# A hybrid decoder layer on one core: two weight staging buffers, another order of the key and query moves, one distance table, sums of squares in the P V pool

## Chip, cores and metric

One core of a Trainium2 chip. The metric is device time of one launch in microseconds (us), the median over runs; lower is better. The profile is of one execution of the kernel.

## The reference, cut to what matters

One layer over 1024 prompt tokens and 8 sampled tokens (one new token each, with key and value caches): an RMS norm, one combined projection to everything that follows, three groups of dilated attention and one sliding-window attention with per-head norms of q and k and an ALiBi penalty, gates, two branch projections, an output projection and a residual.

```python
def project_inputs(x, norm_gain, w_in, qk_norm_a, qk_norm_b):
    h = rms_norm(x, norm_gain)
    parts = jnp.split(jnp.einsum("ntd,de->nte", h, w_in), SPLIT_POINTS, axis=-1)
    ...
def banded_attention(q, k, v, slopes, sinks, max_delta, dist):
    ...
    s = jnp.einsum("nbqgrd,nbkgd->nbgrqk", qb, kk).astype(jnp.float32) * (hd ** -0.5)
    bias = -slopes[:, :, None, None] * (delta * dist)
    p, lse = masked_softmax(s + bias, valid, sink)
    o = jnp.einsum("nbgrqk,nbkgd->nbqgrd", p, vv)
...
# group g of mixer A: windows (128, 512, 2048), dilations (1, 4, 16); weights of the groups from lse
o_a = jnp.einsum("gnth,gnthd->nthd", jax.nn.softmax(lse_a, axis=0), o_a_groups)
a = o_a * silu(z_a); b = o_b * silu(z_b)
mixed = sigmoid(g_a) * (a @ w_branch_a) + sigmoid(g_b) * (b @ w_branch_b)
y = x + mixed @ w_out
```

The caches of the sampled tokens are also written out, shifted by one position.

## The kernel before, in words

The tokens are the columns (1032 of them, in three chunks of 344), features the partitions. Every matrix product in full precision is made of three: both operands are split into a high and a low part (hi and lo), and hi·hi, hi·lo and lo·hi are summed in PSUM. Weights come as 82 tiles of 128 output features (`ORDER`), each 512 KB: 66 of the combined projection, 8 of the branch projections, 8 of the output. `w_load` (L114) has SP load a tile into a staging buffer (`w_st`, one buffer), and `w_conv` (L120) splits it in two halves: ScalarE writes the high part (L126), GpSimd the low part (L127).

A tile and a chunk make a `slot` of 24 matmuls (L248), cut into three *parts* of 8. The program is written in the order of these parts. At the end of each, `part_end` lets the other work in: the attention's three lanes in turn (`stage_s`: S = q·k, L434 or L448/449; `stage_t`: transposes of the probabilities P, L501; `stage_pv`: P V, L543 or L574), everything deferred with `after(parts, f)`, one step of two generators (`dec`, the sampled tokens; `mer`, the combination of the groups), and one piece of the splits of q and k. A unit is one head and some blocks of 128 queries; a job is a pair of heads (head 0, head 1) of a group. Groups 0, 1 and 3 (the sliding window) use `prep_q` and `prep_k`; the third dilated group is `g == 2` and has its own `prep_k2`.

For S, hi and lo of a head are stacked on the partitions: a k tile pair per head (`k_a0`, `k_b0` for head 0, `k_a1`, `k_b1` for head 1), q likewise. The split computes hi and lo for both heads at once, in the rows where they happen to be, and six DMA moves (`move`, L311) of 64 rows each bring the rest to its place. All DMAs (weights, moves, caches, 1 MB copies of the sampled caches at L141, one every six parts) are issued by SP, in program order; a wait of one holds up those behind it.

PSUM has eight banks in three pools: "d" (2) for the dense products, "w" (4) for S, the transposes, sums of squares and small products, "o" (2) for P V. The sum of squares of a q or k chunk (`ssq` in `ev_qk`, L950/951) stays in its bank until `norm` has read it (L230, L960). `evac_o2` empties P V of `g == 2`: two banks, four ScalarE copies (L585/586), two VectorE adds (L590), one GpSimd add (L591). The ALiBi table is loaded per head (`load_tabs`, L1248), and S is turned into penalised scores with it by one VectorE operation (L457, or L437 and L439).

In the main loop the conversion of the next tile and the load of the one after it are placed by hand:

```python
after(1, lambda: w_conv(n + 1, ks=slice(0, 4)))
after(3, lambda: w_conv(n + 1, ks=slice(4, KK)))
after(5, lambda: w_load(n + 2))
```

Of the kernel before, what the change touches and what calls it, by code (L numbers as in the profile page):

```python
# [20 lines left out]
T = 1024  # L21
# [40 lines left out]

def heads(g, c):
    return (2 * c, 2 * c + 1) if g < 3 else (c, 4 + c)
# [3 lines left out]
def hybrid_step(ctx: ExitStack, tc: tile.TileContext, a):  # L68
# [20 lines left out]
    qkg = cst.tile([128, 8], F32, name="qkg")  # L89
    eps = cst.tile([128, 1], F32, name="eps")  # L90
# [6 lines left out]
    nsink = cst.tile([128, 8], F32, name="nsink")  # L97
    nc.vector.memset(eps, EPS)
# [54 lines left out]
    def rt(name):  # L153
        return bp.tile([128, TT], F32R, tag="B", bufs=18, name=name)

    def ft(name):
        return bp.tile([128, TT], F32, tag="B", bufs=18, name=name)
# [45 lines left out]
    def h_root(j):  # L203
        pm = psum("w", 4)
# [108 lines left out]
    def prep_q(j):  # L313

        j.sq = [rt("q_st") for _ in range(2)]
        t = rt("q_lo")
# [19 lines left out]
    def prep_k2(j):  # L336
# [3 lines left out]
        def piece(y):  # L340
            v = j.k[:, :T].rearrange("p (s r) -> p r s", r=16)[:, 8 * y:8 * y + 8].rearrange("p (b w) s -> p b w s", w=2)
            t0, t1 = [side(j.sk[h][y]) for h in range(2)]
            t4 = t0.rearrange("p b l (w s) -> p b l w s", s=64)
            nc.scalar.activation(t4[:, :, 0], v, AF.Copy)
            nc.vector.tensor_tensor(t4[:, :, 1], v, t4[:, :, 0].bitcast(F32), op=ALU.subtract)
# [4 lines left out]
            after(1, lambda: mv(t1, lo_rows, 0, t0, hi_rows, 0))  # L350
            after(1, lambda: mv(t1, hi_rows, 1, t0, hi_rows, 0))
            after(2, lambda: mv(t1, lo_rows, 1, t0, hi_rows, 1))
            after(2, lambda: mv(t1, hi_rows, 0, t0, hi_rows, 1))
            after(5, lambda: mv(t0, hi_rows, 1, t0, lo_rows, 0))
            after(5, lambda: mv(t0, hi_rows, 0, t0, lo_rows, 1))
# [3 lines left out]
    def prep_k(j):  # L359
# [5 lines left out]
        def piece(half):  # L365
            c = part_of(j, half)
            v = j.view(j.k[:, :T])[:, c]
            h = j.view_o(a0[:, :T])[:, c]
            nc.scalar.activation(h, v, AF.Copy)
            nc.vector.tensor_tensor(j.view_o(b0[:, :T])[:, c], v, h.bitcast(F32), op=ALU.subtract)  # L370
            if half:
                after(1, lambda: move(a1, lo_rows, a0, hi_rows))
                after(1, lambda: move(b1, hi_rows, a0, hi_rows))
                after(2, lambda: move(a1, hi_rows, b0, hi_rows))
                after(2, lambda: move(b1, lo_rows, b0, hi_rows))
                after(5, lambda: move(b0, hi_rows, a0, lo_rows))
                after(5, lambda: move(a0, hi_rows, b0, lo_rows))
# [3 lines left out]
    def prep_v(j, half):  # L381
# [3 lines left out]
        pt = psum("w", 4)  # L385
# [36 lines left out]
    def stage_s(u):  # L422
# [3 lines left out]
        if j.g == 2:  # L426
            bias = tab3[:, hd]
            for x in range(2):
                pt = psum("w", 4)
# [8 lines left out]
                for y in range(2):  # L438
                    nc.vector.tensor_tensor_reduce(out=p[:, y], in0=pv[:, y, 0], in1=p[:, y], scale=-0.125, scalar=3e38,  # L439
# [3 lines left out]
        pt = psum("w", 4)  # L443
# [49 lines left out]
    def stage_t(u):  # L493
# [5 lines left out]
        pt = psum("w", 4)  # L499
# [7 lines left out]
        def split():  # L507
            if j.g == 2:

                u.pt = pts[u.base % 3]  # L510
                t = u.pt[:, :T].rearrange("p (b l q) -> p b l q", l=2, q=128)
# [966 lines left out]
```

## Time and profile before

| | us |
|---|---|
| median of three runs | 1244.9 (1244.15 to 1245.51) |
| the profiled execution | 1248.59 |
| its span | 1246.0 |
| TensorE busy (matmul) | 1181.5 |
| ScalarE, VectorE, GpSimd busy | 730.4, 707.0, 606.3 |
| mean granted clock of TensorE | 0.977 of full speed |

The span is the time from the first to the last instruction in the trace of that execution. Busy times of the engines overlap each other. TensorE runs at one of two levels, 2.4 GHz (granted clock 1.00) or 1.2 GHz (0.50).

### The profile page before, as it was taken

The numbers are of one execution on the slowest core, as the hardware profiler recorded it, in microseconds if no ns is written. First come the engines' busy times: TensorE is split into PE (matmuls) and PEld (weight loads), VectorE is DVE, ScalarE is ACT, GpSimd is POOL, SyncE is SP. The second block draws the span as 40 slices with busy tenths as digits, with TensorE's granted clock in tenths as the row PEclk, the third lists the DMA queues.
The fourth block names the chain that finished last, engine by engine and source line by source line (L and its number), as shares of the span: only waits on it lengthen the run. The fifth ranks groups of instructions, "written<-read, shape, count | busy, mean of one in ns | idle before, by whom it ended". The sixth has DMA issues, their size and how long they took to land.

```text
span 1246.0 us, 21929 instructions
## 1 busy us (share of the span) xinstructions
PE 1181.5 (95%) x7625; PEld 1154.4 (93%) x7625; DVE 707.0 (57%) x1714; ACT 730.4 (59%) x1830; POOL 606.3 (49%) x681
## 2 busy tenths in 40 slices
PE   7899999999999998989998989989899999999998
PEld 6799999999899988979987989989899989999998
DVE  5852454676667475766755865757855564333111
ACT  5644675776758584758755677847686522443110
POOL 3554243443535455746363853638554685444220
PEclk9999999999999998989998989989999998999999
DMA  7047557675684849667775859486688754543343
GB/s 224 35 145 224 175 195 223 195 228 149 221 266 166 254 145 279 194 168 220 213 227 177 241 191 264 143 262 195 182 258 228 238 178 161 187 145 110 111 147 100
DMA packets 127278, 238.83 MB, mean 192 GB/s; under 512 B 28648, under 2 KB 102208, under 8 KB 125760
## 3 DMA queue, kind: packets, MB, share of 16 engines
q1 hardware_dynamic: 127168, 237.43, 62.3%
q8 instruction: 60, 0.98, 0.3%
q14 instruction: 50, 0.41, 0.1%
HBM read 180.14 MB, written 113.25 MB: 235 GB/s over the span
## 4 chain that ended last, share of the span: by engine, by line
PE 73%; DMA 7%; DVE 6%; POOL 5%; ACT 4%; issue 4%; SPq 1%; POOLq 0%; DVEq 0%; ACTq 0%
PE ps_d L248 55%; PE ps_w L248 4%; DMA k_a<-k_b 3%; PE ps_w L501 3%; PE ps_o L574 2%; PE ps_w L448 2%; PE ps_w L449 2%; DMA k_b<-k_b 2%; DMA w_st<-in_w 1%; ACT P L467 1%; PE ps_o L248 1%; DVE n_t L726 1%; POOL q_lo L324 1%; POOL n_t L591 1%; PE ps_w L950 1%
## 5 line engine op out<-in xcount | busy, mean ns | idle before, releaser
L248 PE MATMUL ps_d<-h_hi,w 128*128 128x344 f32 x3456 | 867.7, 327 | 12.2 <-DVE sq L1122 5.7
L248 PEld LDWEIGHTS ps_d<-h_hi,w 128*128 128x128 f32 x3456 | 611.7, 193 | 17.1 <-ACT h_hi L191 6.7
L248 PE MATMUL ps_d<-h_lo,w 128*128 128x344 f32 x1728 | 573.2, 332 | 5.9 <-POOL h_lo L221 3.3
L248 PEld LDWEIGHTS ps_d<-h_lo,w 128*128 128x128 f32 x1728 | 332.2, 192 | 10.6 <-POOL h_lo L221 5.8
L127 POOL TENSOR_TENSOR w<-w_st,w 128x512 fp32r<-128x512 f32 (+1 forms) x159 | 211.1, 1330 | 208.3 <-ACT w L126 193.4
L126 ACT ACTIVATE w<-w_st 128x512 fp32r<-128x512 f32 (+1 forms) x160 | 100.3, 631 | 113.3 <-DMA w_st<-in_w 112.5
L467 ACT ACTIVATE P<-P,st 128x256 f32<-128x256 f32 (+1 forms) x256 | 115.6, 453 | 65.6 <-DVE st L457 59.4
L956 POOL TENSOR_TENSOR qn<-qn,rn 128x344 f32<-128x344 f32 x48 | 45.6, 949 | 151.6 <-ACT rn L226 139.7
L528 DVE TENSOR_TENSOR pt<-ps_w,pt 128x384 fp32r<-128x384 f32 (+1 forms) x112 | 49.4, 441 | 57.7 <-ACT pt L527 57.3
L448 PE MATMUL ps_w<-k_a,q_st 128*128 128x128 f32 (+1 forms) x192 | 51.8, 293 | 29.0 <-DMA k_a<-k_b 14.6
L527 ACT ACTIVATE pt<-ps_w 128x384 fp32r<-128x384 f32 (+1 forms) x112 | 44.1, 394 | 42.8 <-DVE pt L528 36.0
L448 PEld LDWEIGHTS ps_w<-k_a,q_st 128*128 128x128 f32 x192 | 37.6, 196 | 31.0 <-issue 31.0
L501 PE MATMUL ps_w<-ident,P 128*128 128x128 f32 x400 | 62.3, 273 | 3.9 <-DVE pt L528 2.1
L956 POOL TENSOR_TENSOR kn<-kn,rn 128x344 f32<-128x344 f32 x39 | 37.0, 949 | 57.0 <-ACT rn L226 51.8
L941 ACT ACTIVATE sq<-ps_d 128x344 f32<-128x344 f32 x87 | 39.3, 452 | 39.8 <-PE ps_d L248 36.2
L946 DVE TENSOR_TENSOR sql<-sq,sqh 128x344 fp32r<-128x344 f32 x87 | 59.5, 684 | 0.8
L457 DVE CUSTOM_DVE_ANT_0 P<-ps_w,tab 128x256 f32<-128x256 f32 (+1 forms) x128 | 43.4, 375 | 27.4 <-PE ps_w L449 27.2
L501 PEld LDWEIGHTS ps_w<-ident,P 128*128 128x128 f32 x400 | 50.2, 140 | 7.1 <-issue 2.3
L792 POOL TENSOR_TENSOR dkv<-dkv,qb 128x512 f32<-128x512 f32 x32 | 42.4, 1331 | 28.0 <-DMA dkv<-in_ca 9.5
L1174 DVE TENSOR_TENSOR xres<-ps_d,xres 128x344 f32<-128x344 f32 x24 | 12.4, 517 | 76.1 <-PE ps_d L248 44.9
L230 DVE SCALAR_TENSOR_TENSOR ps_w<-ps_w,rt 128x344 f32<-128x344 f32 x87 | 45.2, 520 | 18.0 <-ACT rt L227 17.7
L449 PE MATMUL ps_w<-k_b,q_st 128*128 128x128 f32 (+1 forms) x192 | 53.1, 287 | 0.0
(226 smaller groups left out, 2064.7 us busy)
## 6 DMA issues: line engine op xcount, KB each, us to landing
w_st<-in_w SPq DMA_DIRECT2D x81, 512.0 KB
out_sa<-in_ca SPq DMA_DIRECT2D x16, 1020.0 KB
dkv<-in_ca SPq DMA_DIRECT2D x24, 512.0 KB
q_st<-q_lo SPq DMA_DIRECT2D x32, 256.0 KB
k_st<-k_st SPq DMA_DIRECT2D x48, 128.0 KB
sc<-sc_dr SPq DMA_DIRECT2D x32, 192.0 KB
k_b<-k_a SPq DMA_DIRECT2D x18, 256.0 KB
k_a<-k_b SPq DMA_DIRECT2D x18, 256.0 KB
```

Source lines behind the costliest of these rows:

```text
L126: nc.scalar.activation(wh, s, AF.Copy)
L127: eng.tensor_tensor(wl, s, wh.bitcast(F32), op=ALU.subtract)
L230: nc.vector.scalar_tensor_tensor(ssq, ssq, n * EPS, t, op0=ALU.add, op1=ALU.mult)
L248: nc.tensor.matmul(pt[:, :CH], ops[i][0], ops[i][1], start=(i == 0), stop=(i == N - 1))
L448: nc.tensor.matmul(pt[:, o:o + 128 * nk], j.sq[h][:, q], j.ka[h][:, k], start=True, stop=False)
L449: nc.tensor.matmul(pt[:, o:o + 128 * nk], j.sq[h][:, q], j.sk[h][:, k], start=False, stop=True)
L467: nc.scalar.activation(u.p[:, c], u.p[:, c], AF.Exp, scale=-1.0, bias=st[:, qb, h:h + 1], accum_out=st[:, qb, 2 + h:3 + h])
L501: nc.tensor.transpose(pt[:, o:o + 128], u.p[:, o:o + 128], ident)
L527: nc.scalar.activation(t[:, p0:p0 + m], pt[:, o:o + m], AF.Copy)
L528: nc.vector.tensor_tensor(t[:, 512 + p0:512 + p0 + m], pt[:, o:o + m], t[:, p0:p0 + m].bitcast(F32), op=ALU.subtract)
L946: after(0, lambda: nc.vector.tensor_tensor(sl, s, sh.bitcast(F32), op=ALU.subtract))
L956: nc.gpsimd.tensor_tensor(dst[:, col], dst[:, col], r, op=ALU.mult)
```

## The change

1. The staging tile of the weights has two buffers, and the load of tile n+2 is placed at `after(2)` instead of `after(5)`.
2. The pool of long tiles ("B") has 19 instead of 18.
3. In `prep_q`, `prep_k` and `prep_k2` the split writes other tiles, so that the moves at +1 and +2 (k) or +1 and +3 (q) complete head 0, and those at +7 complete head 1.
4. One table of distances (`tabs`, 384 columns) takes the place of the tables per head; the slope of a head goes into the gain of q (`qg`) and into the scale of the VectorE operation. The slopes are written by 32 small GpSimd memsets at the start.
5. The "w" pool has 3 banks, "o" has 3, and the sums of squares are in "o".
6. P V of `g == 2` goes to one bank in 8 matmuls of 128 columns (before: two banks, 4 of 256), emptied by `evac_o`, which now takes the bank as an argument; `evac_o2` goes.
7. In `merge`, three instead of two parts lie ahead of the second VectorE add of the three-group case.
8. In `dec_cols` a 128x8 product replaces the 128x128 one; the broadcast to 128x128 (`qr`) is a copy in `dec_score`.

```diff
-                stage[n] = wp.tile([128, KK, 128], F32, tag="ws", bufs=1, name="w_st") if s is None else s
+                stage[n] = wp.tile([128, KK, 128], F32, tag="ws", bufs=2, name="w_st") if s is None else s
...
-        return bp.tile([128, TT], F32R, tag="B", bufs=18, name=name)
+        return bp.tile([128, TT], F32R, tag="B", bufs=19, name=name)
...
     def prep_q(j):
-            h = j.view_o(q0[:, :T])[:, c]
+            h = j.view_o(t[:, :T])[:, c]
             nc.scalar.activation(h, v, AF.Copy)
-            nc.gpsimd.tensor_tensor(j.view_o(t[:, :T])[:, c], v, h.bitcast(F32), op=ALU.subtract)
+            nc.gpsimd.tensor_tensor(j.view_o(q1[:, :T])[:, c], v, h.bitcast(F32), op=ALU.subtract)
             if half:
-                after(1, lambda: move(q1, lo_rows, q0, hi_rows))
-                after(3, lambda: move(q1, hi_rows, t, hi_rows))
-                after(3, lambda: move(q0, hi_rows, t, lo_rows))
+                after(1, lambda: move(q0, lo_rows, t, lo_rows))
+                after(3, lambda: move(q0, hi_rows, q1, lo_rows))
+                after(7, lambda: move(q1, lo_rows, t, hi_rows))
...
     def prep_k(j):
-            h = j.view_o(a0[:, :T])[:, c]
+            h = j.view_o(b1[:, :T])[:, c]
             nc.scalar.activation(h, v, AF.Copy)
-            nc.vector.tensor_tensor(j.view_o(b0[:, :T])[:, c], v, h.bitcast(F32), op=ALU.subtract)
+            nc.vector.tensor_tensor(j.view_o(a1[:, :T])[:, c], v, h.bitcast(F32), op=ALU.subtract)
             if half:
-                after(1, lambda: move(a1, lo_rows, a0, hi_rows))
-                after(1, lambda: move(b1, hi_rows, a0, hi_rows))
-                after(2, lambda: move(a1, hi_rows, b0, hi_rows))
-                after(2, lambda: move(b1, lo_rows, b0, hi_rows))
-                after(5, lambda: move(b0, hi_rows, a0, lo_rows))
-                after(5, lambda: move(a0, hi_rows, b0, lo_rows))
+                after(1, lambda: move(a0, lo_rows, b1, lo_rows))
+                after(1, lambda: move(b0, hi_rows, b1, lo_rows))
+                after(2, lambda: move(a0, hi_rows, a1, lo_rows))
+                after(2, lambda: move(b0, lo_rows, a1, lo_rows))
+                after(7, lambda: move(a1, lo_rows, b1, hi_rows))
+                after(7, lambda: move(b1, lo_rows, a1, hi_rows))
...
     def stage_s(u):
-            bias = tab[:, hd, 256 - 128 * nk:]
+            bias = tab[:, 256 - 128 * nk:]
-            nc.vector.tensor_tensor_reduce(out=u.p[:, c], in0=pt[:, c], in1=bias, scale=-0.125, scalar=init,
+            nc.vector.tensor_tensor_reduce(out=u.p[:, c], in0=pt[:, c], in1=bias, scale=-0.125 * slope_of(hd), scalar=init,
...
     def stage_pv(u):
         if g == 2:
-            pts2 = [psum("o", 2) for _ in range(2)]
-            for x, pt in enumerate(pts2):
-                for y in range(2):
-                    b = 2 * x + y
-                    v0 = 256 * b + 128 * h
-                    nc.tensor.matmul(pt[:, 256 * y:256 * y + 256], j.vv[i][:, v0:v0 + 128], u.pt[:, 256 * b:256 * b + 256],
-                                     start=(y == 0), stop=True, skip_group_check=True)
-            evac_o2(u, pts2)
+            pt = psum("o", 3)
+            for b in range(4):
+                v0 = 256 * b + 128 * h
+                for n in range(2):
+                    nc.tensor.matmul(pt[:, 128 * b:128 * b + 128], j.vv[i][:, v0:v0 + 128],
+                                     u.pt[:, 512 * n + 128 * b:512 * n + 128 * b + 128],
+                                     start=(b == 0 and n == 0), stop=True, skip_group_check=True)
+            evac_o(u, i, pt)
...
     def merge(...):
                 nc.gpsimd.tensor_tensor(sc[:, 1], sc[:, 1], sc[:, 2], op=ALU.add)
-                yield 2
+                yield 3
                 nc.vector.tensor_tensor(nv, nv, sc[:, 1], op=ALU.add)
...
     def ev_qk(kind, g, c, ch, pt):
         def ssq():
-            pm = psum("w", 4)
+            pm = psum("o", 3)
...
-                after(5, lambda: w_load(n + 2))
+                after(2, lambda: w_load(n + 2))
```

The SP queue around the moves of one k job of group 1 (k tiles `k_a0`, `k_a1`, `k_b0`, `k_b1`), which issues in this order; before:

```order
L311 DMA k_a1_6314<-k_a0_6313 64x1024
L311 DMA k_b1_6316<-k_a0_6313 64x1024
L311 DMA k_a1_6314<-k_b0_6315 64x1024
L311 DMA k_b1_6316<-k_b0_6315 64x1024
L970 DMA out_pa1<-v_t_6218 128x512
L735 DMA o_dr_92<-n_t_4064 128x256
L141 DMA out_sa2<-in_ca2 16x16384
L311 DMA k_b0_6315<-k_a0_6313 64x1024
L311 DMA k_a0_6313<-k_b0_6315 64x1024
L118 DMA w_st_6543<-in_w 128x1024
```

And after the change:

```order
L322 DMA k_a0_6343<-k_b1_6346 64x1024
L322 DMA k_b0_6345<-k_b1_6346 64x1024
L322 DMA k_a0_6343<-k_a1_6344 64x1024
L322 DMA k_b0_6345<-k_a1_6344 64x1024
L963 DMA out_pa1<-v_t_6251 128x512
L695 DMA sc_6441<-sc_dr_144 64x3x256 x2
L724 DMA o_dr_126<-n_t_4106 128x256
L129 DMA w_st_6491<-in_w 128x1024
L152 DMA out_sa2<-in_ca2 16x16384
L322 DMA k_a1_6344<-k_b1_6346 64x1024
L322 DMA k_b1_6346<-k_a1_6344 64x1024
```

The four moves ahead of the 1 MB copy now write head 0's tiles, the two behind it head 1's, and the load of a weight has moved ahead of the copy and of the last two moves.

TensorE at a P V unit of `g == 2` with a sum of squares (`sqh`, `sql`) behind it and a column of the sampled tokens (`qx`); before:

```order
L248 MATMUL ps_d_5290<-h_hi_90,w_5040 128x344
L543 MATMUL ps_o_5347<-pt_1378,v_5062 128x256 x2
L543 MATMUL ps_o_5348<-pt_1378,v_5062 128x256 x2
L950 MATMUL ps_w_5360<-sqh_5273,blk_76 128x344
L951 MATMUL ps_w_5360<-sql_5274,blk_76 128x344
L784 MATMUL ps_w_5370<-ident_71,qx_4172 128x128
```

And after the change:

```order
L259 MATMUL ps_d_5334<-h_hi_124,w_5078 128x344
L550 MATMUL ps_o_5391<-pt_1412,v_5102 128x128 x8
L943 MATMUL ps_o_5404<-sqh_5317,blk_76 128x344
L944 MATMUL ps_o_5404<-sql_5318,blk_76 128x344
L777 MATMUL ps_w_5414<-ident_71,qr_5332 128x128
```

The unit's four matmuls on two banks became eight on one, and the sum of squares that follows takes its bank from the same pool.

## Rows read from the trace of the kernel before

**Rows 1.** The page, part 4: share of the span by engine in the last chain.

```profile
PE 73%; DMA 7%; DVE 6%; POOL 5%; ACT 4%; issue 4%; SPq 1%; POOLq 0%; DVEq 0%; ACTq 0%
```

**Rows 2.** Waits of TensorE: line, what it waited for: us, times, longest us.

```profile
PE ps_w L448 <- DMA k_a<-k_b: 14.6, 4, 6.0
PE ps_w L448 <- issue: 14.3, 4, 5.3
PE ps_d L248 <- DVE sq L1122: 5.7, 2, 3.0
...
PE ps_w L748 <- DVE v L393: 2.7, 1, 2.7
...
PE ps_w L844 <- DVE dmx L840: 2.4, 1, 2.4
PE ps_w L501 <- DVE pt L528: 2.1, 1, 2.1
PE ps_w L501 <- ACT sls L789: 1.6, 1, 1.6
```

**Rows 3.** Timeline of the SP queue, 526 to 550 us: start, us, line, DMA.

```profile
537.06 0.74 SPq L141 DMA_DIRECT2D out_sa<-in_ca  x1
538.80 0.47 SPq L311 DMA_DIRECT2D k_b<-k_a  x1
539.36 1.53 SPq L311 DMA_DIRECT2D k_a<-k_b  x1
```

**Rows 4.** The chain, 526 to 552 and 876 to 893 us: start, us, what.

```profile
533.72 5.01 DMA k_b<-k_b
...
539.36 9.92 DMA k_a<-k_b
...
875.85 5.13 DMA k_b<-k_b
```

**Rows 5.** Windows, two stalls: us; busy PE, PEld, DVE, ACT, POOL; clock, DMA share, GB/s.

```profile
543.30:549.50 6.20, 0.20 (x2) 0.11 (x1) 2.16 (x4) 2.84 (x6) 1.26 (x2) 0.89 0.98 229
...
891.00:891.60 0.60, 0.08 (x2) 0.08 (x1) 0.18 (x1) 0.60 (x2) 0.00 (x0) 1.00 0.13 55
```

**Rows 6.** The longest of six windows behind stalls, and their sum; clock 0.50 in all.

```profile
665.00:671.00 6.00, 6.00 (x21) 5.61 (x22) 1.60 (x6) 1.51 (x5) 1.27 (x1) 0.50 1.03 404
...
sum 26.70, PE 26.64 PEld 25.90 DVE 12.17 ACT 9.11 POOL 9.05; mean PE 4.44 PEld 4.32 DVE 2.03 ACT 1.52 POOL 1.51
```

**Rows 7.** Waits of the SP queue, and of ScalarE.

```profile
SPq L118 <- POOL w L127: 178.0, 37, 12.1
...
ACT w L126 <- DMA w_st<-in_w: 112.5, 28, 10.4
```

**Rows 8.** TensorE by line and shape: count, busy us, mean ns, idle before.

```profile
L543 PE MATMUL ps_o<-pt,v 128*128 128x256 f32 x64 | 10.8, 289 | 1.5 <-DVE ot L590 1.5
```

**Rows 9.** Sums: 653.9-657.3 with 814.35-817.8, and 1019.15-1022.6 with 1036.2-1043; clock 0.50-0.51.

```profile
sum 6.85, PE 6.85 PEld 6.85 DVE 4.12 ACT 2.36 POOL 2.34; mean PE 3.42 PEld 3.42 DVE 2.06 ACT 1.18 POOL 1.17
...
sum 10.25, PE 10.25 PEld 10.20 DVE 5.16 ACT 2.27 POOL 5.68; mean PE 5.12 PEld 5.10 DVE 2.58 ACT 1.13 POOL 2.84
```

**Rows 10.** Timeline of VectorE, around 1012 us.

```profile
1011.64 6.40 DVE L726 TENSOR_TENSOR n_t<-n_t,sc 128x256 f32<-128x256 f32 x1
```

**Rows 11.** Timeline of TensorE, 305 to 312 us.

```profile
305.11 0.64 PE L574 MATMUL ps_o<-pt,v 128*128 128x256 f32 x4
305.58 0.32 PE L950 MATMUL ps_w<-sqh,blk 128*128 128x344 f32 x1
...
310.74 0.85 PE L574 MATMUL ps_o<-pt,v 128*128 128x128 f32 x6
311.43 0.32 PE L950 MATMUL ps_w<-sqh,blk 128*128 128x344 f32 x1
```

**Rows 12.** Timeline of TensorE and of VectorE, 715 to 718 us.

```profile
715.06 0.32 PE L950 MATMUL ps_w<-sqh,blk 128*128 128x344 f32 x1
...
717.28 0.52 DVE L960 SCALAR_TENSOR_TENSOR qn<-ps_w,qn 128x344 f32<-128x344 f32 x1
```

More of the change, by code (lines that the diff above doesn't have):

```diff
@@ L60, with slope_of @@
 ORDER = tile_order()
+def slope_of(h):
+    return 2.0 ** -(h + 1)
 def heads(g, c):
@@ L89, in hybrid_step @@
     qkg = cst.tile([128, 8], F32, name="qkg")
+    slope = cst.tile([128, 2, 8], F32, name="slope")
+    qg = cst.tile([128, 16], F32, name="qg")
     eps = cst.tile([128, 1], F32, name="eps")
@@ L97, in hybrid_step @@
     nsink = cst.tile([128, 8], F32, name="nsink")
+    for x in range(8):
+        for i, h in enumerate(heads(x // 4 * 3, x % 4)):
+            nc.gpsimd.memset(slope[64 * i:64 * i + 64, 0, x:x + 1], 1 / slope_of(h))
+            nc.gpsimd.memset(slope[64 * i:64 * i + 64, 1, x:x + 1], slope_of(h) / 8)
     nc.vector.memset(eps, EPS)
@@ L153, in rt @@
     def rt(name):
-        return bp.tile([128, TT], F32R, tag="B", bufs=18, name=name)
+        return bp.tile([128, TT], F32R, tag="B", bufs=19, name=name)
     def ft(name):
-        return bp.tile([128, TT], F32, tag="B", bufs=18, name=name)
+        return bp.tile([128, TT], F32, tag="B", bufs=19, name=name)
     ap2 = tc.alloc_tile_pool(name="att", bufs=1, reuse_waits="tile")
@@ L442, in stage_s @@
             return
-        pt = psum("w", 4)
+        pt = psum("w", 3)
         o = 0
@@ L567, in stage_pv @@
             if first:
-                ob[half] = psum("o", 2)
+                ob[half] = psum("o", 3)
             pt = ob[half]
@@ L575, in stage_pv @@
                                  start=(first and n == 0), stop=True, skip_group_check=True)
-    def evac_o2(u, pts2):
-        j, h = u.j, u.h
-        if j.n is None:
-            j.n = ft("n_t")
-        t, t2 = [tmp(k, [s, 512])[:64].rearrange("p (x b q) -> p x b q", x=2, q=128) for k, s in (("ot", 64), ("ot2", 128))]
-        n = j.n[64 * h:64 * h + 64, 512 * u.i:512 * u.i + 512].rearrange("p (x b q) -> p x b q", x=2, q=128)
-        vs = [pt.rearrange("p (b l q) -> p b l q", l=2, q=128) for pt in pts2]
-        for x in range(2):
-            nc.scalar.activation(t[:, x], vs[x][64:128, :, 0], AF.Copy)
-            nc.scalar.activation(t2[:, x], vs[x][0:64, :, 1], AF.Copy)
-        def add():
-            for x in range(2):
-                nc.vector.tensor_tensor(t2[:, x], vs[x][0:64, :, 0], t2[:, x], op=ALU.add)
-            nc.gpsimd.tensor_tensor(n, t, t2, op=ALU.add)
-        after(1, add, True)
     def evac_o1(u, pt):
@@ L608, in evac_o1, with evac_o @@
         after(1, add, True)
-    def evac_o(u, half):
+    def evac_o(u, half, pt):
         j, h = u.j, u.h
-        pt = ob.pop(half)
         if j.n is None:
@@ L938, in ev_qk @@
         col = slice(ch * CH, (ch + 1) * CH)
-        gc = 2 * g + (kind == "k")
+        gn = qg[:, 4 * g + c:4 * g + c + 1] if kind == "q" else qkg[:, 2 * g + 1:2 * g + 2]
         s = tmp("sq", [128, CH])
         nc.scalar.activation(s, pt[:, :CH], AF.Square)
-        nc.vector.tensor_scalar(dst[:, col], pt[:, :CH], qkg[:, gc:gc + 1], None, op0=ALU.mult)
+        nc.vector.tensor_scalar(dst[:, col], pt[:, :CH], gn, None, op0=ALU.mult)
         sh = tmp("sqh", [128, CH], F32R)
@@ L1238, in conv_consts @@
         nc.vector.tensor_copy(blk, blk_f)
-        nc.vector.tensor_scalar(hsel, blk_f[:, ::64], 0.125, None, op0=ALU.mult)
+        nc.vector.tensor_copy(hsel, blk_f[:, ::64])
         nc.vector.tensor_scalar(qkg, qkg, -1.0 / 128, None, op0=ALU.mult)
+        for g in range(4):
+            nc.vector.tensor_scalar(qg[:, 4 * g:4 * g + 4], slope[:, 0, 4 * (g // 3):4 * (g // 3) + 4], qkg[:, 2 * g:2 * g + 1], None, op0=ALU.mult)
         nc.vector.tensor_scalar(nsink, psink, -1.0, None, op0=ALU.mult)
     def load_tabs():
-        for i in range(3):
-            tf = ft("tab_f")
-            src = a["tab"][:, 4 * i:4 * i + 4] if i < 2 else a["tab3"]
-            dst = tab[:, 4 * i:4 * i + 4] if i < 2 else tab3
-            nc.sync.dma_start(tf[:, :1024], src.rearrange("p h k -> p (h k)"))
-            after(4 + 9 * i, lambda dst=dst, tf=tf: nc.vector.tensor_copy(dst.rearrange("p h k -> p (h k)"), tf[:, :1024]))
+        tf = ft("tab_f")
+        nc.sync.dma_start(tf[:, :256], a["tab"][:, 0])
+        nc.sync.dma_start(tf[:, 256:384], a["tab3"][:, 0])
+        after(4, lambda: nc.vector.tensor_scalar(tabs, tf[:, :384], 1 / slope_of(0), None, op0=ALU.mult))
     NW = 4
```

91 lines of the change are left out of this document (46 added, 45 removed).

## Prediction

> **What bounds the kernel now.** First the page: the chain that ended last is 73% PE [rows 1]. So most of the time is matmul issue, which the change hardly touches. The largest share of the rest is DMA, 7%. The question is therefore where TensorE stands still and for what, and the waits by engine answer it [rows 2]: the largest two are one place, the first S matmul of a unit (L448), 14.6 + 14.3 = 28.9 us in eight stalls, half of them with the move k_a<-k_b named, half with nothing that the profile could name ("issue"). The other groups that I use below sum to less than 6 us each.
>
> The queue shows why [rows 3]. SP issues the four moves of head 1, the last at 533.72, then a 1 MB copy out_sa<-in_ca at 537.06, and only then, at 538.80 and 539.36, the two moves that complete head 0. Head 0 is what S reads first. In the chain [rows 4] that last of the first four takes 5.01 us to land, and k_a<-k_b, behind the copy, 9.92 us. TensorE stands from 543.3 to 549.4, and in that window VectorE is busy 2.16, ScalarE 2.84 and GpSimd 1.26 of 6.2 us [rows 5]: no other engine is waiting to become the bound there.
>
> A stall is paid twice. After six of the eight, TensorE's granted clock is 0.50, so 1.2 GHz of its 2.4, for up to 6 us of dense work. Six windows laid over these stretches sum to 26.7 us with PE busy in all but 0.06 of it [rows 6]; the same work at the full clock takes half, so 13.3 us are lost.
>
> **The change part by part.** The profiled execution took 1248.6 us; the median of three runs is 1244.9, so 3.7 is taken off at the end.
>
> *Splits and moves.* Now the first four moves complete head 0, and head 1's two follow at +7 parts. The four are issued where head 1's were: by [rows 4] the last of them landed at 533.72 + 5.01 = 538.73 and, in the last place of the seven, at 875.85 + 5.13 = 880.98; TensorE arrived at 543.3 and 891.0 [rows 5]. Head 1 has the rest of head 0's parts, of some 1.3 us each, to get its two. The eighth stall is a q move, whose place at +3 parts stays; I keep 2.6 us for it, less than an average stall. With 2 us more for places where the queue is longer than in these two, 4.6 of 28.9 stay: **-24.3**. Bounds: 0 (every first pair lands just too late as well) and -28.9.
>
> *Their half clock.* Five or six of the stretches go, 13.3 less 1.3: **-12.0**, bounds 0 and -13.3.
>
> *Two staging buffers.* SP's queue waited 178.0 us in 37 waits for GpSimd's half of the conversion (L118 <- L127), because the next weight could only be loaded when the one buffer was free, and everything behind it in SP's order stood too; ScalarE waited 112.5 us for weights [rows 7]. With two buffers and the load at after(2), neither wait is needed. What TensorE gains is bounded by the waits that hang on late loads or on the backlog behind them: L748 2.7 (the ml load was issued late), L844 2.4, L501 behind sls 1.6 and pt 2.1, L543 1.5 [rows 2, 8], 10.3 in all, and the half clock behind two of them, 6.85 us of busy time [rows 9], so 3.4. Of these 13.7 I take 9: the pt wait lies behind VectorE's own work: **-9**, bounds 0 and -13.7.
>
> *The tail.* Two stalls of L248 behind sq L1122, 5.7 us [rows 2], come from a VectorE add of 6.40 us at 1011.64 beside running GpSimd work [rows 10]; with their half clock of 10.25 us [rows 9] they cost 5.7 + 5.1 = 10.8. The add's yield of 3 instead of 2 moves it relative to L1122, and what it meets there is open. I take **-2**, bounds +3 (another row of the same kind stands in its way, 3.0 was the longest wait) and -10.8.
>
> *P V of the third group.* 16 units (64 matmuls at 4 each [rows 8]) take 8 matmuls of 128 columns instead of 4 of 256. Four of 256 columns start at 305.11 and the next instruction at 305.58: 0.47 us. Six of 128 columns start at 310.74 and are followed at 311.43: 0.69 us, so eight take 0.92 [rows 11]. 16 x 0.45 = **+7.2**, bounds 0 (if only columns counted) and +7.2. The Trainium skill ("TensorE: Matmul & The Clock Gate", Back-to-back issue gap) gives about 81 ns for a matmul of 128 columns in a stream; by that estimate eight take 0.65 us and the sum is 4.3 us lower. The rows' 115 ns for each of the six stands against it, and I keep the rows.
>
> *Their evacuation.* ScalarE's four copies, VectorE's two adds and GpSimd's one become one longer copy and one VectorE add per unit, and the wait for GpSimd's buffers goes. TensorE waited 1.5 us in all behind this evacuation [rows 8], already counted: 0 here, covered as long as ScalarE does not lag.
>
> *PSUM.* "w" loses a bank, and the 87 sums of squares leave it for "o", which gains one. An ssq tile lives until L960 has read it: the matmul of the next one comes at 715.06, the read of an earlier one starts at 717.28 and takes 0.52 [rows 12]. With three banks of "o" for P V and ssq, that next one falls on the earlier one's bank and waits 717.80 - 715.06 = 2.7 us. I found no other place so late, but several under 0.8 us. I take two waits of the large size: **+5**, bounds 0 and +10.
>
> *Tables, memsets, decode columns.* The 32 small memsets stand at the start of GpSimd's program, where it waits for the first weight. The small qx and the copy qr instead of one 128x128 operation lie on GpSimd, which loses the 16 adds of the evacuation. **0**, bounds 0 and +1.
>
> Sum: -24.3 - 12.0 - 9 - 2 + 7.2 + 5 = -35.1. 1248.6 - 35.1 - 3.7 = **1209.8**.
>
> **The rivals.**
>
> *Half the gain (1225).* A transfer is late whatever the order: moves take 5.0 us to land even in front of the copy [rows 4], and with the loads issued earlier the queue holds more when they start. If each of seven places keeps 1.5 us of stall (10.5, of which 2 are counted) and half of the half clock (6 more), that is +14.5: 1224.3. For it: the DMA share in the window of the longest stall is 0.98 [rows 5]. Against it: TensorE arrived 4.6 and 10.0 us after the first four had landed. The Trainium skill ("DMA: Bandwidth & Descriptors", Queues, rings and completion order) says that each DMA engine consumes a ring's descriptors in ring order. By that the copy in front, not the place among the moves, makes 9.92 of 5.01, and a weight load pulled ahead of the last moves would do the same to them; [rows 3, 4] agree as far as the copy goes.
>
> *All goes (1190).* The q move, the late pairs, the loads' backlog and the tail cost nothing any more: -4.6 - 1.3 - 4.7 - 8.8 = -19.4, so 1190.4. Against it: L501's pt wait lies behind VectorE's work, which stays, and one extra part before the tail's add need not lead to a better place.
>
> *Slower (1255).* With three banks the S tiles and transposes (some 240 tiles) find their bank not yet read. The one such wait with four banks, L501 behind pt, was 2.1 us [rows 2]. If one tile in ten waits so long, 24 x 2.1 = 50 us, less the 5 counted: 1255. It decides from 20 such waits (42 us, the gain of 35 and the 5 counted). Against it: now there is one, and the 87 ssq tiles, each held until L960 has read it, leave "w". The Trainium skill ("Perfetto Trace Analysis", Optimizing Tensor Performance, Matmuls) asks that independent groups rotate through different banks and prefers larger matmuls; by that rule both edits on P V and "w" point this way. No run here shows three banks.
>
> *It doesn't do what it says (1243).* SP may still hold the first four moves behind something, so that the stalls stay as they are, while P V costs its 7.2 and the other edits give 9: 1243.
>
> **How the numbers follow.** Forecast 0.55, half gain 0.25, all goes 0.12, no real change 0.03, slower 0.05. Runs of this kernel lie within 1.4 us of each other, so about 0.2% (2.5 us) can be told from no change. Faster by over that: 0.93; within it: 0.02; slower: 0.05. The likeliest case's own range, from the PSUM and tail bounds and an uncounted P V cost, is 1200 to 1219; with the half gain and most of "all goes" the range is 1192 to 1229.
>
> **What would show it.** Right: L448's waits for k moves under 6 us in all; no half clock behind them; P V's eight matmuls at 0.92 us; SP's L118 waits for L127 gone. Wrong: L448 or L387 wait for something new; a sum of ps_w or ps_o waits above 10 us; head 1's last moves named as releaser; ScalarE or VectorE near full in stretches where they were at half.

## The result, and the profile after

The changed kernel takes 1207.2 us (median of four runs, 1205.5 to 1209.0) where the kernel before, beside it, takes 1245.2. The ratio, taken over all these runs and not from the two medians, is 0.9688, with a 95% interval of 0.9661 to 0.9716. The profiled execution took 1207.7 us, its span is 1205.9, and the mean granted clock of TensorE is 0.990 (before 0.977).

The span is 40.1 us shorter than that of before (1246.0). TensorE's busy time and the share of engines in the last chain, from parts 1 and 4 of the page of the changed kernel (against [rows 1]):

```profile
PE 1169.6 (97%) x7689; PEld 1148.6 (95%) x7689; DVE 689.8 (57%) x1700; ACT 718.8 (60%) x1782; POOL 580.7 (48%) x713
...
PE 88%; DVE 5%; DMA 3%; issue 2%; ACT 1%; POOL 1%; SPq 0%; DVEq 0%; POOLq 0%
```

Busy time fell from 1181.5 to 1169.6, so 11.9 us of the 40.1 were work that now runs faster or is not there. The other 28.2 us were idle time of TensorE. DMA was 7% of the chain and is 3%.

Where TensorE still waits, in the changed kernel (line, what it waited for: us, times, longest), against [rows 2]:

```profile
PE ps_o L943 <- DVE qn L953: 9.9, 3, 5.0
...
PE ps_d L259 <- DVE sq L1115: 5.6, 2, 3.5
...
PE ps_w L398 <- DVE v L404: 2.9, 3, 1.8
...
PE ps_o L943 <- DVE n_t L595: 0.8, 1, 0.8
```

The first S matmul (now L459) is not in the list at all: 28.9 us of stalls are gone, the one for a q move among them. The waits of L844 and L748, and the one for `sls`, are gone as well. The tail's two stalls (now L1115) are what they were, 5.6 against 5.7. New is the sum of squares L943, which waits for the norm that reads its bank: 9.9 us in three places.

What the queue now does around the same k job, in the timeline of SP (start, us, line, DMA), against [rows 3]:

```profile
503.78 0.56 SPq L152 DMA_DIRECT2D out_sa<-in_ca  x1
515.83 0.50 SPq L322 DMA_DIRECT2D k_a<-k_b  x1
...
520.32 2.22 SPq L695 DMA_DIRECT2D sc<-sc_dr  x2
...
524.81 0.89 SPq L322 DMA_DIRECT2D k_a<-k_b  x1
```

After the copy at 503.78 SP issues nothing until 515.83. It holds the first move of head 0, and what it waits for is an S matmul of the job before: the move's target tile takes the place of one that S still reads. The loads of the merge weights (sc) stand behind it until 520.32. The waits of SP (same columns as above) name this, and what the second staging buffer did, against [rows 7]:

```profile
SPq L322 <- PE ps_w L459: 29.1, 3, 12.4
...
SPq L129 <- POOL w L138: 21.8, 6, 7.2
```

And ScalarE's wait for weights:

```profile
ACT w L137 <- DMA w_st<-in_w: 6.9, 6, 1.9
```

The time that SP's weight loads wait for GpSimd's conversion fell from 178.0 to 21.8 us, ScalarE's wait for a weight from 112.5 to 6.9. In their place comes L459 as the reader that a move waits for, 29.1 us in three waits (one line of S was waited for before too, L449, 19.7 in four).

The chain from 515 to 531 us (start, us, what) shows how the late sc load reaches TensorE:

```profile
521.61 7.07 DMA sc<-sc_dr
...
528.78 0.42 DVE n_t L715
...
529.87 0.53 DVE qn L953
...
530.53 0.63 PE ps_o L943
```

The load lands at 528.7. VectorE, which wants it for L715, stands until then; the norm (L241, L953) is behind L715 in its queue; the bank is free at 530.4 and the sum of squares starts at 530.53, 5.0 us late. The half clock follows such a stall as it did before. Four windows are laid over the half clock after 500 us; here are the first of them and their sum (us; busy PE, PEld, DVE, ACT, POOL; clock, DMA share, GB/s), against [rows 6, 9]:

```profile
529.10:535.90 6.80, 5.37 (x20) 5.40 (x21) 4.86 (x13) 4.92 (x12) 5.51 (x7) 0.50 1.15 371
...
sum 17.00, PE 15.57 PEld 15.60 DVE 11.84 ACT 11.43 POOL 14.11; mean PE 3.89 PEld 3.90 DVE 2.96 ACT 2.86 POOL 3.53
```

Before, the ten windows of [rows 6, 9] held 43.7 us of such work; these four hold 15.6. None of them follows a k move: two follow L943's long waits, one follows waits of 1.8 and 0.8 us for VectorE, one the tail. A fifth stretch, at 54.6 to 61.5 us with a clock of 0.51, lies ahead of the attention; the trace of the same kernel in run 9 has none there.

P V of the third group, eight matmuls of 128 columns, and what starts after them, in TensorE's timeline, against [rows 11]:

```profile
444.69 1.00 PE L550 MATMUL ps_o<-pt,v 128*128 128x128 f32 x8
445.53 0.37 PE L943 MATMUL ps_o<-sqh,blk 128*128 128x344 f32 x1
```

The next instruction starts 0.84 us after the first of the eight; four of 256 columns took 0.47.

### The profile page after: what moved, and what is told of

The parts are those of the page before. It is cut to its first block, busy times and chain, and to the rows that moved or that the text cites. A ratio compares the mean times of both kernels' runs of the same rounds, so it can differ in the third digit from the quotient of the medians.

```text
span 1205.9 us, 21988 instructions
## 1 busy us (share of the span) xinstructions
PE 1169.6 (97%) x7689; PEld 1148.6 (95%) x7689; DVE 689.8 (57%) x1700; ACT 718.8 (60%) x1782; POOL 580.7 (48%) x713
## 3 DMA queue, kind: packets, MB, share of 16 engines
q1 hardware_dynamic: 127024, 236.06, 63.9%
## 4 chain that ended last, share of the span: by engine, by line
PE 88%; DVE 5%; DMA 3%; issue 2%; ACT 1%; POOL 1%; SPq 0%; DVEq 0%; POOLq 0%
PE ps_d L259 67%; PE ps_w L259 4%; PE ps_w L512 3%; PE ps_o L582 2%; DMA sc<-sc_dr 2%; PE ps_w L460 2%; PE ps_w L459 2%; PE ps_o L943 1%; PE ps_o L944 1%; PE ps_o L550 1%; PE ps_o L259 1%; PE ps_w L398 1%; PE ps_w L445 1%; DVE dpr L904 1%; DVE x L226 1%
## 5 line engine op out<-in xcount | busy, mean ns | idle before, releaser
L259 PE MATMUL ps_d<-h_hi,w 128*128 128x344 f32 x3456 | 859.0, 324 | 12.2 <-ACT h_hi L202 6.0
L259 PEld LDWEIGHTS ps_d<-h_hi,w 128*128 128x128 f32 x3456 | 604.1, 190 | 16.4 <-ACT h_hi L202 6.8
L259 PEld LDWEIGHTS ps_d<-h_lo,w 128*128 128x128 f32 x1728 | 328.7, 190 | 10.5 <-POOL h_lo L232 5.7
L1167 DVE TENSOR_TENSOR xres<-ps_d,xres 128x344 f32<-128x344 f32 x24 | 12.4, 517 | 76.1 <-PE ps_d L259 45.8
L939 DVE TENSOR_TENSOR sql<-sq,sqh 128x344 fp32r<-128x344 f32 x87 | 54.6, 627 | 1.0
L241 DVE SCALAR_TENSOR_TENSOR ps_o<-ps_o,rt 128x344 f32<-128x344 f32 x87 | 45.2, 519 | 17.1 <-ACT rt L238 16.9
L460 PE MATMUL ps_w<-k_b,q_st 128*128 128x128 f32 (+1 forms) x192 | 52.0, 282 | 0.0
L335 POOL TENSOR_TENSOR q_st<-qn,q_hi 128x512 fp32r<-128x512 f32 x32 | 45.1, 1428 | 11.0 <-ACT q_hi L334 10.4
L938 ACT ACTIVATE sqh<-sq 128x344 fp32r<-128x344 f32 x87 | 42.8, 492 | 11.5 <-PE ps_o L943 9.1
```

What stands on the lines that cost most here:

```text
L241: nc.vector.scalar_tensor_tensor(ssq, ssq, n * EPS, t, op0=ALU.add, op1=ALU.mult)
L259: nc.tensor.matmul(pt[:, :CH], ops[i][0], ops[i][1], start=(i == 0), stop=(i == N - 1))
L335: nc.gpsimd.tensor_tensor(j.view_o(q1[:, :T])[:, c], v, h.bitcast(F32), op=ALU.subtract)
L460: nc.tensor.matmul(pt[:, o:o + 128 * nk], j.sq[h][:, q], j.sk[h][:, k], start=False, stop=True)
L939: after(0, lambda: nc.vector.tensor_tensor(sl, s, sh.bitcast(F32), op=ALU.subtract))
```

## The experiments

Twelve runs follow, each beside the kernel before on the same chip. That kernel took 1251.6 us beside runs 1 to 4, 1249.1 beside 5 to 8 and 1249.7 beside 9 to 12, so runs of different groups are compared by their ratio to it and not by their times. In the texts of the expectations theory A is the order of the moves, rival B the staging buffer. The changed kernel's ratio, 0.9688, is what the ratios of its variants are held against; 0.001 is 1.25 us. Line numbers are those of each run's own kernel: the first S matmul, L459 in the changed kernel, is L460 in runs 4, 8 and 12 and L448 in run 5.

**1. The old splits and moves in the changed kernel.** `prep_q`, `prep_k` and `prep_k2` are those of before:

```diff
-                after(1, lambda: move(a0, lo_rows, b1, lo_rows))
...
-                after(7, lambda: move(b1, lo_rows, a1, hi_rows))
+                after(1, lambda: move(a1, lo_rows, a0, hi_rows))
...
+                after(5, lambda: move(a0, hi_rows, b0, lo_rows))
```

> The changed kernel with the splits and moves of before (head 1's tiles completed first, head 0's last moves at +5 and +3), all else as changed. Theory A (the order of the moves removed the stalls of the first S matmul): 20 to 29 us of those stalls come back, with 8 to 12 us of half clock behind them, so 1235 to 1247 us. Rival B (the second staging buffer and the earlier load freed the queue, so that the moves land early in any order): under 10 us of these stalls come back, 1207 to 1217 us.

1241.4 us (1239.0 to 1242.2), ratio 0.9916 (0.9889 to 0.9943). Waits of TensorE:

```profile
PE ps_w L459 <- DMA k_a<-k_b: 19.8, 7, 4.6
...
PE ps_w L459 <- issue: 1.2, 1, 1.2
```

21.0 us of stalls at the first S matmul come back, all but 1.2 with the move named, and the time rises by 0.0228, some 28 us. Theory A holds, rival B falls: with two staging buffers the old order still stalls.

**2. One staging buffer, load at +5, in the changed kernel.**

```diff
-                stage[n] = wp.tile([128, KK, 128], F32, tag="ws", bufs=2, name="w_st") if s is None else s
+                stage[n] = wp.tile([128, KK, 128], F32, tag="ws", bufs=1, name="w_st") if s is None else s
...
-                after(2, lambda: w_load(n + 2))
+                after(5, lambda: w_load(n + 2))
```

> The changed kernel with one staging buffer and the load at +5 parts, as before; moves as changed. Theory A: the first S matmul still waits for no k move; only waits on late loads and the backlog behind them come back, 4 to 14 us, so 1211 to 1221 us. Rival B: the queue is blocked again, the moves land late, 1230 us or more.

1221.4 us (1217.4 to 1224.9), ratio 0.9761 (0.9729 to 0.9793): 0.0073 or 9 us slower than the changed kernel. SP waits for GpSimd's conversion as before,

```profile
SPq L129 <- POOL w L138: 163.0, 35, 12.6
```

and ScalarE for weights,

```profile
ACT w L137 <- DMA w_st<-in_w: 115.3, 32, 10.8
```

but k moves hold S for only 0.2 us. With the rest of the change in place, the buffer is worth what the prediction gave it.

**3. Sums of squares back in w.**

```diff
-            pm = psum("o", 3)
+            pm = psum("w", 4)
```

with 4 banks in all uses of "w" and 2 in all uses of "o".

> The changed kernel with the sums of squares back in the pool w (4 banks, o with 2). Theory: the 9.9 us for which the sum of squares waits for the norm that reads its bank go, with some 5 us of half clock behind two of these waits, and waits of w tiles of at most 5 us come: 1195 to 1207 us. Rival (VectorE's norm is late anyway, and the bank of w that it holds then stops S or the transposes): the same 10 us show on other lines, 1203 to 1212 us. Rival (two banks of o are too few for P V): 1212 us or more, waits at ps_o.

1206.6 us (1205.0 to 1210.4), ratio 0.9648 (0.9622 to 0.9674). The interval overlaps that of the changed kernel. Waits of TensorE:

```profile
PE ps_w L944 <- DVE sql L939: 9.0, 5, 4.6
```

The wait for the norm's bank is gone, and 9.0 us stand at the second matmul of the sum of squares, which waits for VectorE to make its low part. That looks like the first rival (VectorE is late, and the bank decides only where that shows), but it is so for less than half. VectorE's timeline:

```profile
539.11 3.78 DVE L939 TENSOR_TENSOR sql<-sq,sqh 128x344 fp32r<-128x344 f32 x1
```

The longest wait, 4.6 us, stands behind this one subtraction, which takes 0.52 us in the median; it is told of in the last section. At the three places where the changed kernel waited 9.9 us for the bank, 1.4 us each are left. By ratio the run is 0.004 (5 us) below the changed kernel, with intervals that overlap, and 1206.6 us lies in the ranges of both, so the time does not decide between the theory and this rival. The second rival (two banks of o too few for P V) falls.

**4. The k moves of the second dilated group 3 parts later.**

```diff
             if half:
+                d = 3 if j.g == 1 else 0
-                after(1, lambda: move(a0, lo_rows, b1, lo_rows))
+                after(1 + d, lambda: move(a0, lo_rows, b1, lo_rows))
...
```

and so on for the other five.

> The changed kernel with the k moves of the second dilated group placed 3 parts later (+4, +5, +10). In three of its jobs SP stands some 12 us at the first move, because the move's target tile is still read by the S matmuls of the job before; the loads of the merge weights queue behind it, VectorE waits for them, and with it the norm that frees the bank of the sum of squares. Theory: with the moves later, SP issues these loads about 8 us earlier, VectorE's wait of 4.8 us and the 9.9 us of TensorE go, with most of the half clock behind them: 1192 to 1200 us. Rival (the loads are slow in themselves, 7 us from issue to landing wherever they stand, or the norm waits for something else next): 1204 to 1209 us. Rival (the moves now land too late for S): first S matmuls wait again, 1210 us or more.

1200.9 us (1198.6 to 1205.1), ratio 0.9602 (0.9574 to 0.9630), below the changed kernel's interval. Waits of TensorE:

```profile
PE ps_o L944 <- DVE qn L954: 4.1, 3, 1.8
...
PE ps_w L460 <- DMA k_a<-k_a: 0.9, 1, 0.9
```

VectorE's wait for the sc load:

```profile
DVE n_t L716 <- DMA sc<-sc_dr: 7.5, 3, 2.6
```

VectorE's wait for sc, 14.9 us in five places in the changed kernel, is 7.5 in three, and TensorE's wait for the norm fell from 9.9 to 4.1. So the late load was the cause of more than half of it. In one place the moves now come too late for S (0.9 and, on the other tile, 0.6 us).

**5. The moves alone, in the kernel before.** The edit is the reverse of that of run 1, made in the kernel before.

> The kernel before with nothing of the change but the splits and moves. Theory A: the seven stalls for k moves go (26 us) and most of the half clock behind them (11 us); the single staging buffer still blocks the queue in places, so a few us of them may stay: 1208 to 1222 us where the kernel before takes 1245. Rival B (the moves need the second staging buffer and the earlier load to land in time): 10 us or more of stalls stay, 1225 us or more.

1240.5 us (1238.0 to 1242.7), ratio 0.9926 (0.9902 to 0.9949): only 9 us. The k stalls are gone, as theory A said, but TensorE is idle for as long as in the kernel before (span 1237.4 less 1173.5 busy is 63.9, before 64.5). What was gained is busy time, 8.0 us of it, as the granted clock rose from 0.977 to 0.991; of the stalls themselves 0.6 us were. Waits of TensorE in the attention:

```profile
PE ps_w L951 <- DVE sql L946: 8.5, 8, 4.1
...
PE ps_w L501 <- ACT P L467: 5.7, 6, 2.5
PE ps_w L501 <- DVE pt L528: 3.3, 3, 2.1
```

The waits for the low part of the sum of squares, for P and for its transpose pt grew as the others went; L951's was 0.6 before, and L501 did not wait for P at all. Two waits of ScalarE in the same run:

```profile
ACT w L126 <- DMA w_st<-in_w: 117.5, 30, 10.4
ACT P L467 <- DVE st L457: 70.7, 51, 7.3
```

ScalarE still waits for weights as before, with its other work queued behind; that this is what makes TensorE wait is a reading that run 10 puts to the test. The time came out as rival B said, by another way: the moves don't land late, the other engines are late.

**6. 18 long tiles in the changed kernel.** `bufs=19` becomes 18 in `rt` and `ft`.

> The changed kernel with 18 long tiles instead of 19. It serves as the base of the next run and tells what the nineteenth is worth. Theory: the first moves wait for tiles that are still read, and one tile less makes them wait longer, or makes a split on ScalarE or VectorE wait: 1207 to 1220 us. Rival: the pool is not what they wait for, 1205 to 1210 us.

1214.6 us (1212.7 to 1214.9), ratio 0.9716 (0.9698 to 0.9734), 3.5 us above the changed kernel; the intervals overlap. TensorE's busy time on the page:

```profile
PE 1171.3 (97%) x7689; PEld 1149.3 (95%) x7689; DVE 690.4 (57%) x1700; ACT 718.1 (59%) x1782; POOL 579.7 (48%) x713
```

Two of its waits:

```profile
PE ps_o L943 <- DVE qn L953: 6.5, 3, 2.9
...
PE ps_w L459 <- issue: 5.1, 1, 5.1
```

A new stall of 5.1 us at the first S matmul, with no releaser named, agrees with the theory, that a move waits longer for its tile: SP's second k move of that job stands 6.9 us for an S matmul and goes out at 352.04, while in the changed kernel it follows the first within a microsecond.

**7. The same, with P V of the third group as before.**

```diff
-            pt = psum("o", 3)
-            for b in range(4):
...
-            evac_o(u, i, pt)
+            pts2 = [psum("o", 3) for _ in range(2)]
+            for x, pt in enumerate(pts2):
+                for y in range(2):
...
+            evac_o2(u, pts2)
```

with the splits for it in `stage_t`.

> As the run with 18 long tiles, and P V of the third group with its splits and evacuation as before: two banks of o, four matmuls of 256 columns, four copies of ScalarE, two adds of VectorE, one of GpSimd. Theory (eight matmuls of 128 columns cost TensorE 0.37 us per unit more than four of 256): TensorE's busy time falls by 16 x 0.37 = 5.9 us; against the run with 18 tiles the time falls by 2 to 6 us, less what the heavier evacuation and the two banks of o give back. Rival (the evacuation and the banks are worth more than the matmuls): 2 us or more slower than the run with 18 tiles.

1222.4 us (1221.2 to 1231.1), ratio 0.9800 (0.9756 to 0.9844): 7.7 us slower than run 6 by the medians. The busy time on the page:

```profile
PE 1168.4 (96%) x7625; PEld 1142.2 (94%) x7625; DVE 698.7 (57%) x1716; ACT 730.2 (60%) x1830; POOL 602.4 (49%) x729
```

TensorE's waits:

```profile
PE ps_o L964 <- DVE qn L974: 11.3, 8, 4.0
...
PE ps_o L964 <- DVE kn L974: 1.7, 2, 1.2
```

TensorE is busy 2.9 us less, and idle 10.8 us more (1220.9 - 1168.4 = 52.5 against 1213.0 - 1171.3 = 41.7). The sum of squares waits for a norm in ten places instead of three, 13.0 us instead of 6.5. The rival holds: evacuation and banks together are worth more than the matmuls. Which of the two it is, the run does not separate. P V that takes two of three banks comes round sooner to the bank that a norm still holds. But ScalarE's four copies also stand ahead of the root that the norm needs (ScalarE's timeline, third group):

```profile
605.56 0.38 ACT L595 ACTIVATE ot<-ps_o 64x256 f32<-64x256 f32 x1
...
607.05 0.53 ACT L236 ACTIVATE rn<-ps_o,eps 128x344 f32<-128x344 f32 x1
```

That is 1.5 us from the first copy to the root, where run 6 with its one copy has 0.6. And 9.4 of the 13.0 us lie at the three places of the late sc load, where no P V of the third group runs.

**8. Later moves (2 parts) and sums of squares in w.** Runs 3 and 4 together, with `d = 2`.

> The k moves of the second dilated group 2 parts later (+3, +4, +9), and the sums of squares in w (4 banks, o with 2). Theory: with the merge's loads issued earlier VectorE is late by less than 2 us, so a bank held by the norm stops nobody any more: the waits at ps_o for the norm (4.1 us with the later moves alone) and the first S matmul's 1.5 us for the moves go, 1193 to 1200 us where the changed kernel takes 1207. Rival (VectorE's lateness shows at the sums of squares' low part instead, as when ssq alone was put in w): same as the later moves alone, 1197 to 1203 us.

1201.4 us (1199.0 to 1203.4), ratio 0.9612 (0.9590 to 0.9634), the same as run 4. One wait of TensorE is left of those in question:

```profile
PE ps_w L945 <- DVE sql L940: 6.7, 4, 4.1
```

By the time the rival holds. By the trace, the longest of the four waits (4.1) stands again behind one subtraction (L940), of 3.8 us at 535.67; the other three are 2.6 us together.

**9. The changed kernel again**, beside the last three.

> The changed kernel itself, as the base for the three runs beside it: 0.969 of the kernel before, within 0.003.

1206.2 us (1202.1 to 1215.8), ratio 0.9669 (0.9604 to 0.9733). The wait of L943 for the norm is 10.3 us in three places, as it was.

**10. Moves, staging buffer and small tables, the rest as before.** The edits of runs 3, 6, 7 and 11 together in the changed kernel.

> The moves, the second staging buffer and the small tables of the change, but the banks (4 of w, 2 of o, sums of squares in w), P V of the third group with its evacuation, 18 long tiles and the yield of 2 as before. The moves alone took the stalls for k moves away and gave most of it back as waits for ScalarE and VectorE all over the attention. Theory (those waits come from the weights that ScalarE waits 117 us for, with its other work queued behind): with the second buffer they go, 1215 to 1225 us where the kernel before takes 1245. Rival (they come from the work on ScalarE, VectorE and GpSimd itself, which the change lightens by the evacuation of the third group and the banks): 1228 us or more.

1220.0 us (1216.4 to 1222.0), ratio 0.9765 (0.9713 to 0.9817). Two waits of ScalarE:

```profile
ACT P L478 <- DVE st L468: 70.6, 53, 7.3
...
ACT w L137 <- DMA w_st<-in_w: 10.4, 8, 2.4
```

Moves, buffer and small tables together are worth some 29 us (0.0235), where the moves alone gave 9, and the time is within what the theory said. The rest of the change (P V, banks, the tile, the yield) gives 0.0077, some 10 us.

Run 2 has to be read beside this. It has the moves and that rest, but one staging buffer, and it reaches 0.9761, the same as this run's 0.9765, though ScalarE waits 115.3 us for weights in it. So next to the moves either the buffer or the rest gives some 20 us (0.9926 less 0.9765 or 0.9761), and the second of the two to come gives 9 or 10. The buffer is enough to make the moves pay, as the theory said, but it is not the only way, so the wait for weights is not shown to be the one cause; ScalarE's wait for st is as long here as in run 5. Both runs also have the small tables, which no run takes alone; GpSimd's busy time, 601.8 us in run 5 and 601.5 here, gives no sign that they matter.

**11. The merge's yield of 2 in the changed kernel.**

```diff
-                yield 3
+                yield 2
                 nc.vector.tensor_tensor(nv, nv, sc[:, 1], op=ALU.add)
```

> The changed kernel with the yield of 2 ahead of the merge's second add. Theory: the tail's two stalls (5.6 us) are the same with both, and the add's place matters little in the attention: within 3 us of the changed kernel. Rival (VectorE waits for GpSimd's sum when the add comes one part earlier, and its queue stands): 3 to 8 us slower.

1197.8 us (1195.5 to 1201.8), ratio 0.9584 (0.9524 to 0.9644). Beside it the changed kernel's four runs were 1202.1 to 1215.8: no run overlaps, 8.4 us between the medians, though the intervals of the two ratios do overlap. Neither expectation had this: it is *faster*. The timeline of SP around the same k job:

```profile
507.52 1.26 SPq L695 DMA_DIRECT2D sc<-sc_dr  x2
...
509.55 0.49 SPq L322 DMA_DIRECT2D k_a<-k_b  x1
516.54 0.49 SPq L322 DMA_DIRECT2D k_b<-k_b  x1
```

One part earlier, the merge's add lets the sc load be issued at 507.52, ahead of the moves, of which the first goes out at 509.55 and the second stands until 516.54; in the changed kernel the load came behind them, at 520.32. Waits of TensorE:

```profile
PE ps_d L259 <- DVE sq L1115: 7.4, 3, 3.0
...
PE ps_o L943 <- DVE qn L953: 2.1, 3, 1.3
```

The norm's bank costs 2.1 us instead of 9.9, while the tail is somewhat worse (7.4 against 5.6 in the changed kernel and 4.0 in run 9).

**12. Later moves by 2 parts, sums of squares in o.** Run 4 with `d = 2`.

> The changed kernel with the k moves of the second dilated group 2 parts later instead of 3 (+3, +4, +9), sums of squares in o. Theory: SP still issues the merge's loads ahead of the moves, and the moves land before S needs them: 0.958 to 0.963 of the kernel before. Rival (two parts are too few, SP stands at the move again): 0.964 to 0.969.

1196.7 us (1194.7 to 1197.6), ratio 0.9579 (0.9530 to 0.9629). TensorE's wait for the norm:

```profile
PE ps_o L944 <- DVE qn L954: 3.9, 3, 1.6
```

SP's wait for S:

```profile
SPq L322 <- PE ps_w L461: 3.0, 2, 1.9
```

SP's moves wait 3.0 us for S instead of 29.1. By its median this is the fastest version that ran, 9.5 us under the changed kernel beside it. Run 11's yield together with these moves was not tried.

## Why the prediction was right, and where it was not

The forecast was 1210, the time 1207.2. The main mechanism held: the order of the moves ended the stalls. That the sum came so near is partly luck. The yield cost where a gain was put down, P V gained where a cost was put down, the long tile had no term, and the largest two terms hold only together with the rest of the change.

- *Splits and moves, and their half clock* (-24.3 and -12.0). Right as a mechanism: the stalls went, 28.9 us in the trace, and came back with the old order (run 1: 21.0 us of stall, some 28 us of time); no half clock that is left follows a k move. What failed is the sentence of the first part that no other engine was waiting to become the bound. In the window of one stall none was; but in run 5, with the stalls gone, TensorE waits as long as before for ScalarE and VectorE, which had used the stalls to catch up. Alone the moves give 9 us, 8 of it the busy time that the half clock had cost and almost nothing of the stalls; with the second buffer and the small tables 29 (run 10), with the rest of the change and one buffer 30 (run 2). The terms were added as if each stood by itself, and they don't.
- *Two staging buffers* (-9). Measured 9 by run 2, with all else in place. Next to the moves alone it is some 20, small tables included (run 10 against run 5).
- *The tail* (-2). 5.7 us of stalls became 5.6 (4.0 in run 9); with a yield of 2 they are 7.4 (run 11), so the yield helps there by some 2 or 3 us. But one part was enough to put the sc loads behind a move that stands for 12 us, and taken as a whole the yield of 3 costs 8.4 us by run 11. The term looked at what the add meets on VectorE and not at the DMA whose issue waits for the add. And the queue was read as if moves issued at once, which the trace of before does not show either; after the move at 526.48 the next stands for an S matmul:

```profile
526.48 0.50 SPq L311 DMA_DIRECT2D k_a<-k_a  x1
532.54 0.50 SPq L311 DMA_DIRECT2D k_b<-k_a  x1
```

- *P V of the third group* (+7.2) *and its evacuation* (0). The matmuls cost 0.84 - 0.47 = 0.37 us per unit, so 5.9; the sixfold run of [rows 11] over-priced it a little, and the estimate of 0.65 us for eight, from the 81 ns of the Trainium skill ("TensorE: Matmul & The Clock Gate", Back-to-back issue gap), is further off, on the other side. The evacuation was the error. Taken as a whole the edit gains 7.7 us (run 7 against run 6), with the sums of squares in "o"; no run prices it against the old banks. "Already counted: 0" looked at the waits that TensorE already had behind this evacuation, and not at the sums of squares, which now wait behind its banks and its copies.
- *PSUM* (+5). The waits are 9.9 + 0.8 us, with half clock behind the long ones. Run 3, which takes the edit back, is 5 us faster by ratio, with intervals that overlap, as other waits come in their place; so the size may be right. One of the two long waits is the place that [rows 12] shows, but the reason is not the bank alone: runs 4, 11 and 12 cut the wait by more than half without touching a bank. The bank was held long because VectorE stood for a load.
- *Long tiles*: 19 instead of 18 had no term. Run 6 puts it near 3.5 us, within the overlap of two intervals.

The slower rival (three banks of w) did not show: no wait at a w tile is larger than before, apart from 2.9 us at L398. But of the signs of being wrong one came, and another in part: the waits at ps_w and ps_o sum to 15.1 us (9.9 + 2.9 + 1.5 + 0.8), above 10, most of it behind the late load; and L398, which was L387, waits 2.9 us for v, where it had waited 0.2.

The prediction read the Trainium skill's rule ("Perfetto Trace Analysis", Optimizing Tensor Performance, Matmuls), which asks for rotating banks and prefers larger matmuls, as pointing to a slower kernel. On TensorE the larger matmuls are the cheaper ones, 0.47 against 0.84 us per unit, but the kernel with them, and with the two banks and the evacuation that go with them, is 7.7 us slower (run 7).

"Half the gain" foresaw that moves would still be late in the queue. They were late (SP stands up to 12.4 us at the first of them, in three places), yet it was not S that paid for it but the loads behind them.

Left open: what the buffer and the rest of the change each take away of run 5's waits, and whether the small tables have a part in it; why run 6's tile is worth what it is, place by place; and what runs 11 and 12 would give together.

## What to carry to other kernels

A stall that is removed can also have been the time in which other engines caught up (here 29 us of stalls gave 9 when removed alone): before its length is counted as gain, look at the waits of those engines all along the stage and not in the window of the stall, and try the removal alone and with whatever else lightens them. When a DMA is moved on an in-order queue, ask first what its *target* still has to wait for, since everything issued behind it pays; here two parts later, or one load one part earlier, were worth 8 to 10 us. And price an evacuation by all that queues behind it, behind its banks and behind its copies, and not only by the waits that already show.

## What was not expected of the hardware

A VectorE subtraction of 128x344 with both inputs in SBUF takes 0.52 us in the median, and in one place of run 5 it took 6.44, with TensorE waiting 4.1 us for it. The group over the whole run (ns: min, median, max), and the instruction itself:

```profile
L946 DVE TENSOR_TENSOR sql<-sq,sqh x87: 495/517/6440, 74.1 to 901.5; 128x344 fp32r<-128x344 f32 x87
```

```profile
556.95 6.44 DVE L946 TENSOR_TENSOR sql<-sq,sqh 128x344 fp32r<-128x344 f32 x1
```

GpSimd in the same time, three of its eight rows, the last of them included:

```profile
556.41 1.27 POOL L127 TENSOR_TENSOR w<-w_st,w 128x512 fp32r<-128x512 f32 x1
...
560.04 2.97 POOL L324 TENSOR_TENSOR q_st<-qn,q_hi 128x512 fp32r<-128x512 f32 x2
562.98 0.72 POOL L916 TENSOR_TENSOR rw<-rw 8x128 f32<-8x128 f32 x1
```

VectorE's instruction ends at 563.4, 0.4 us after the second of these (560.04 + 2.97 = 563.0), while the last, on 8 partitions, still runs; in a window over it GpSimd is busy without a gap. The 6.40 us of [rows 10] and the 3.8 us behind the waits of runs 3 and 8 are of the same kind. The Trainium skill ("SBUF — State Buffer", SBUF: two separate sides) says that VectorE instructions with two SBUF inputs and GpSimd share a pair of ports, and that whoever starts first has it for the whole instruction while the other blocks. The trace agrees in that VectorE's instruction is long while GpSimd works; here it was long for a run of GpSimd instructions and not for one, and what let it through beside the last of them is not shown. No run here took the GpSimd work away to show the cause.
